# Low halves of 32 weight tiles written by ScalarE and an adding transfer instead of VectorE, and eight convolution slices per tile

## The chip, the core and the metric

The kernel runs on one core of a Trainium2 chip. The metric is the device time of one execution in microseconds (us). Engines are named as in the profile: PE (TensorE matrix multiplies), PEld (its weight loads), DVE (VectorE), ACT (ScalarE), POOL (GpSimd), SP (SyncE, which only issues transfers here).

## The reference, cut to what matters

One decoder layer over 1024 positions of width 1024, all in float32: a mixer (an input projection whose columns feed four heads of causal differential attention and a gated convolution of width 31), a cross-attention into 256 memory tokens, a gated feed-forward part and a final norm. The change touches only how the weights of the input projection and of the memory projection are prepared:

```
proj = jnp.einsum("bsd,dc->bsc", h, w_in)        # q, k, v and 2 x 512 convolution columns
c = u[..., :CV_WIDTH] * jax.nn.sigmoid(u[..., CV_WIDTH:])
c = causal_dwconv(c, cv_dw_w) + cv_dw_b          # width 31
...
kv = jnp.einsum("bmd,de->bme", m, w_ckv)         # 256 memory tokens, 2048 columns
```

## The kernel before, in words

Each float32 product is made of three passes on TensorE in the rounded format fp32r: a weight tile `raw` (128x1024, 512 KB) is split into `whi` (the value rounded to fp32r) and `wlo = raw - whi`, and `mm3` (L196 to L200) multiplies hi by lo, lo by hi and hi by hi. `split_w` (L174) makes the two halves: ACT copies raw into `whi` (L181), then DVE subtracts (L182). There are two buffers each of `whi` and `wlo` and three of `raw`, so the split of a tile can begin only when TensorE has finished the tile two places ahead of it, and it must be done when TensorE reaches the tile itself. `need(kind, m)` hands out a prepared tile and has the next one loaded (by SP, L171) and split.

The tiles come in the order of the list `seq`. The input projection has 16 ("in", order `in_order`; the first two are split in quarters by other code), then 4 for the values ("v", `vproj`), 16 for the memory ("kv", called kv0 to kv15 here, `mem_kv`, each 24 multiplies of 256 columns), and later "out", "cq", "co" and "dn".

The stages that matter:

- From about 60 to 232 us the projections run: one tile takes 48 multiplies of 512 columns. DVE meanwhile empties their results and runs the depthwise convolution `conv31`, cut into slices of one instruction of some 0.74 us (L371). `run_bg(NBG)` takes NBG slices after each tile, at a lower priority than the rest (17 such calls); `run_bg(1000)` takes what is left after `vproj`.
- From 232 to about 430 us the differential attention runs. TensorE's order is written out by hand: in each step scores (L695 to L698), transposes, weighted sums, and pieces of `mem_kv` as filler between them. DVE takes row maxima (L708), combines (L734 to L738) and empties the memory products (`mb`, L628; a single PSUM buffer, so the next pair of kv tiles waits for it). ACT takes exponentials (L714) and copies. POOL has small chains for norms (L779 to L783 and L814 to L816).

The order within ACT, DVE, POOL and SP is made by a scheduler ahead of time, from priorities and its own estimate of durations; on the chip each engine and each queue goes strictly in that order, and an instruction that waits holds up everything behind it.

Of the kernel before, what the change touches and what calls it, by code (L numbers as in the profile page):

```python
# [14 lines left out]
ALU = mybir.AluOpType  # L15
# [42 lines left out]
def hybrid_block_kernel(ctx: ExitStack, tc: tile.TileContext, xT, memT, pos, vecs, lams, ropec,  # L58
                        wi, wv, wo, wq, wkv, wc, wu, wd, gfin, outT, outB):
    nc = tc.nc  # L60
# [15 lines left out]
    def nm(s):  # L76
        cnt[0] += 1
        return f"{s}_{cnt[0]}"

    def R():  # L80
        return pt.tile([P, S], F32R, tag="t", name=nm("r"))
# [4 lines left out]
    def T(dt=F32):  # L86
        return pt.tile([P, S], dt, tag="t", name=nm("t"))
# [19 lines left out]
    def f(ap):  # L107
        return ap.bitcast(F32)
# [34 lines left out]
    in_order = [12, 8, 0, 1, 13, 9, 2, 3, 14, 10, 4, 5, 6, 7, 15, 11]  # L143
# [30 lines left out]
    def split_w():  # L174
        kind, m, mode, raw = loaded.pop(0)
        if mode == "rd":
            hi, lo = R(), R()
        else:
            hi = pw[0].tile([P, S], F32R, tag="whi", name=nm("whi"), bufs=2)
            lo = pw[0].tile([P, S], F32R, tag="wlo", name=nm("wlo"), bufs=2)  # L180
        nc.scalar.copy(out=hi, in_=raw)  # L181
        nc.vector.tensor_tensor(out=lo, in0=raw, in1=f(hi), op=ALU.subtract)  # L182
        prepped[(kind, m)] = (hi, lo)

    def need(kind, m, ahead=None):
# [5 lines left out]
    def load_to(i):  # L191
        while wpos[0] <= min(i, wend[0] - 1):
            load_w()
            split_w()
# [65 lines left out]
    for i in range(2):  # L260
        kind, m, src, _ = seq[wpos[0]]
        wpos[0] += 1
        raw = pw[0].tile([P, S], F32, tag="raw", name=nm("raw"), bufs=3)
# [67 lines left out]
    def run_bg(n):  # L331
        with tc.high_priority(offset=-500):
            while n > 0 and bg:
                g = bg.pop(0)
                if next(g, StopIteration) is not StopIteration:
                    bg.append(g)
                    n -= 1
# [117 lines left out]
    def rope(tiles):  # L455

        r = T()
        for h in range(NH):
            nc.scalar.dma_start(out=r[h * 32:(h + 1) * 32, :], in_=tiles[h][48:80, :])
        sw = T()  # L460
        nc.vector.stream_shuffle(out=sw, in_=r, mask=SWAP)
        nc.vector.tensor_tensor(out=r, in0=r, in1=cos_t, op=ALU.mult)
        nc.vector.tensor_tensor(out=sw, in0=sw, in1=sin_t, op=ALU.mult)
        nc.vector.tensor_tensor(out=r, in0=r, in1=sw, op=ALU.add)
        for h in range(NH):
            nc.scalar.dma_start(out=tiles[h][48:80, :], in_=r[h * 32:(h + 1) * 32, :])
# [38 lines left out]
                                           in1=rxb[:, sl], op0=ALU.mult, op1=ALU.mult)  # L505
        qk[m] = t

    NBG = 6

    with tc.manual_schedule(engines={mybir.EngineType.PE}):  # L510
        w, w2 = need("in", 12), need("in", 8, 0)
# [27 lines left out]
    for m in in_order[3:]:  # L539
# [6 lines left out]
        else:  # L546
            qk_out(m, [(slice(0, S), ps)])
            if m % 4 == 3:
                rope(qk[m - 3:m + 1])
        run_bg(NBG)  # L550
    vsb = [T() for _ in range(4)]

    def vproj():
# [3 lines left out]
        for i in range(4):  # L557
# [8 lines left out]
            if i < 3:  # L566
                run_bg(NBG)
        for tb in range(NB):
# [277 lines left out]
    next(prep)  # L846
    run_bg(NBG)

# [139 lines left out]
    for m in range(8):  # L988
# [8 lines left out]
        hi, lo = R(), R()  # L997
# [601 lines left out]
```

## Time and profile before

| | us |
|---|---|
| median of three runs | 1416.72 (1414.6 to 1417.54) |
| the profiled execution | 1418.36 |
| its span, first to last instruction | 1416.6 |
| busy: PE / DVE / ACT / POOL | 1378.1 / 1066.8 / 578.1 / 211.2 |

A busy time is the sum of an engine's instructions; matrix multiplies overlap one another, so a full PE stretch shows a busy time equal to its length. The granted clock of TensorE (PEclk) is 1.00 at 2.4 GHz and half of that at 1.2 GHz.

### The profile page before, as it was taken

Reading aid. Unit: us, or ns where it says so; the run is one execution under the profiler, and the core shown is the slowest. Engines: PE = TensorE matmul, PEld = TensorE weight load, DVE = VectorE, ACT = ScalarE, POOL = GpSimd, SP = SyncE. Lnnn points to the kernel's source line nnn. Section 1 sums busy time; section 2 is a strip of 40 time slices with the busy share of each in tenths; the row PEclk is TensorE's granted clock in tenths of the full one; section 3 lists DMA queues with packets and bytes.
Section 4 is the critical chain, followed back from the end, with each engine's and each line's share of the span. In section 5 each row is a group of like instructions: output and inputs, shape, how many; then the busy total and the mean of one; then the engine's idle time right before and its main releaser. Section 6 shows DMA issues by size and latency. Waiting matters only on the chain.

```text
span 1416.6 us, 17449 instructions
## 1 busy us (share of the span) xinstructions
PE 1378.1 (97%) x6709; PEld 1148.2 (81%) x6709; DVE 1066.8 (75%) x1385; ACT 578.1 (41%) x1023; POOL 211.2 (15%) x169
## 2 busy tenths in 40 slices
PE   8999999898899999999999999999999999999998
PEld 6888887887787888888878787887887877888886
DVE  7799999999955424454688888988888897666636
ACT  6211135688763223343464444444443451221213
POOL 0000000013210000000134333443334400000000
PEclk9999999999999999999999999999999999999999
DMA  6132123432205422202421222222222274313103
GB/s 220 42 98 73 56 90 98 141 118 77 74 31 200 149 90 74 75 31 75 155 80 70 76 80 83 89 75 79 85 75 89 89 299 176 119 61 118 45 1 119
DMA packets 50196, 137.36 MB, mean 97 GB/s; under 512 B 6336, under 2 KB 8640, under 8 KB 50112
## 3 DMA queue, kind: packets, MB, share of 16 engines
q1 hardware_dynamic: 43904, 119.98, 25.2%
q10 hardware_dynamic: 6208, 16.26, 3.6%
q8 instruction: 53, 0.87, 0.2%
q14 instruction: 31, 0.25, 0.1%
HBM read 101.51 MB, written 28.41 MB: 92 GB/s over the span
## 4 chain that ended last, share of the span: by engine, by line
PE 61%; DVE 18%; issue 8%; ACT 7%; POOL 6%; DMA 1%; SPq 0%; POOLq 0%; ACTq 0%; DVEq 0%
PE big L198 16%; PE big L200 16%; PE big L199 16%; POOL t L1171 5%; DVE q L1323 4%; ACT q L1321 3%; PE tb L765 2%; DVE r L221 2%; PE bk L198 1%; DVE wu L221 1%; PE bk L200 1%; PE bk L199 1%; PE mb L198 1%; DVE q L1346 1%; DVE q L1298 1%
## 5 line engine op out<-in xcount | busy, mean ns | idle before, releaser
L199 PE MATMUL big<-r,wlo 128*128 128x512 f32 x624 | 243.7, 390 | 0.6 <-DVE wlo L182 0.6
L200 PE MATMUL big<-r,whi 128*128 128x512 f32 x624 | 243.7, 391 | 0.0
L198 PE MATMUL big<-r,whi 128*128 128x512 f32 x560 | 219.7, 392 | 3.1 <-DVE r L304 2.1
L181 ACT CAST whi<-raw 128x1024 fp32r<-128x1024 f32 x58 | 61.4, 1058 | 204.1 <-PE big L200 171.2
L199 PEld LDWEIGHTS big<-r,wlo 128*128 128x128 f32 x624 | 117.6, 188 | 24.8 <-DVE wlo L182 0.9
L200 PEld LDWEIGHTS big<-r,whi 128*128 128x128 f32 x624 | 117.4, 188 | 24.6
L1431 DVE TENSOR_TENSOR t<-t,big 128x1024 f32<-128x1024 f32 x70 | 85.4, 1220 | 61.9 <-PE big L200 61.8
L1323 DVE SCALAR_TENSOR_TENSOR q<-q,vec,q 128x1023 f32<-128x1023 f32 x88 | 112.6, 1280 | 19.9 <-ACT q L1321 19.8
L198 PEld LDWEIGHTS big<-r,whi 128*128 128x128 f32 x560 | 105.6, 189 | 27.0 <-DVE r L304 3.4
L198 PE MATMUL big<-r,r 128*128 128x512 f32 x312 | 121.8, 391 | 1.8 <-DVE t L1431 1.6
L199 PE MATMUL big<-r,r 128*128 128x512 f32 x312 | 121.5, 389 | 0.0
L200 PE MATMUL big<-r,r 128*128 128x512 f32 x312 | 121.5, 389 | 0.0
L198 PE MATMUL ub<-r,wu 128*128 128x512 f32 x302 | 119.0, 394 | 1.7 <-ACT half L1278 1.7
L199 PE MATMUL ub<-r,wu 128*128 128x512 f32 x302 | 117.6, 389 | 0.0
L200 PE MATMUL ub<-r,wu 128*128 128x512 f32 x302 | 117.6, 389 | 0.0
L1171 POOL TENSOR_TENSOR t<-uraw 128x512 f32<-128x512 f32 x22 | 48.4, 2199 | 389.3 <-DMA uraw<-in_wu_dram 167.1
L198 PE MATMUL ub<-r,t 128*128 128x512 f32 x228 | 90.0, 395 | 4.2 <-ACT half L1278 2.8
L199 PE MATMUL ub<-r,t 128*128 128x512 f32 x228 | 88.8, 390 | 0.0
L200 PE MATMUL ub<-r,t 128*128 128x512 f32 x228 | 88.8, 389 | 0.0
L371 DVE SCALAR_TENSOR_TENSOR cv<-t,vec,cv 128x511 f32<-128x511 f32 (+14 forms) x120 | 84.2, 743 | 0.0
L181 ACT CAST r<-raw 128x1024 fp32r<-128x1024 f32 x22 | 22.9, 1051 | 134.8 <-PE big L198 134.5
L182 DVE TENSOR_TENSOR wlo<-raw,whi 128x1024 fp32r<-128x1024 f32 x58 | 70.9, 1223 | 6.8 <-ACT whi L181 6.6
(340 smaller groups left out, 3047.8 us busy)
## 6 DMA issues: line engine op xcount, KB each, us to landing
uraw<-in_wu_dram SPq DMA_DIRECT2D x88, 256.0 KB, 2.9
z_dr<-q SPq DMA_DIRECT2D x22, 512.0 KB, 2.6
raw<-in_wd_dram SPq DMA_DIRECT2D x22, 512.0 KB, 3.7
t<-z_dr SPq DMA_DIRECT2D x22, 512.0 KB, 4.8
raw<-in_wkv_dram SPq DMA_DIRECT2D x16, 512.0 KB, 3.7
raw<-in_wi_dram SPq DMA_DIRECT2D x14, 512.0 KB, 3.7
t<-h_dr SPq DMA_DIRECT2D x9, 512.0 KB, 10.0
kv_dr<-r SPq DMA_DIRECT2D x8, 512.0 KB, 3.5
```

What stands on the lines that cost most here:

```text
L181: nc.scalar.copy(out=hi, in_=raw)
L182: nc.vector.tensor_tensor(out=lo, in0=raw, in1=f(hi), op=ALU.subtract)
L198: nc.tensor.matmul(out, wh, xl, start=start, stop=False, **kw)
L199: nc.tensor.matmul(out, wl, xh, start=False, stop=False, **kw)
L200: nc.tensor.matmul(out, wh, xh, start=False, stop=stop, **kw)
L221: nc.vector.tensor_tensor(out=lo, in0=src, in1=f(hi), op=ALU.subtract)
L371: nc.vector.scalar_tensor_tensor(out=y[:, i:], in0=x[:, :n2 - i], scalar=t, in1=y[:, i:], op0=ALU.mult, op1=ALU.add)
L765: nc.tensor.matmul(av, u["at"][:, bs(j)], vsb[j // 2][:, (j % 2) * HALF + h * P:][:, :P], start=j == 0, stop=j == qb)
L1171: nc.gpsimd.tensor_tensor(out=out, in0=a, in1=b, op=ALU.add)
L1321: nc.scalar.mul(t, u, tp[2])
L1323: nc.vector.scalar_tensor_tensor(out=t[:, d:], in0=u[:, :S - d], scalar=tp[2 - d], in1=t[:, d:], op0=ALU.mult, op1=ALU.add)
L1431: nc.vector.tensor_tensor(out=h2[m], in0=h2[m], in1=ps, op=ALU.add)
```

## The change: what it does

For 32 tiles (the last 12 of "in", the 4 "v" and the 16 "kv") the subtraction on DVE is left out. ACT writes a second tile, `lo = -hi`, and a transfer issued from POOL's queue adds the raw tile to it on the way (`accum_op=ALU.add`), SBUF to SBUF, 512 KB. The sum is the same low half. POOL issued no transfer before. The other tiles keep the subtraction. NBG goes from 6 to 8.

```
         nc.scalar.copy(out=hi, in_=raw)
-        nc.vector.tensor_tensor(out=lo, in0=raw, in1=f(hi), op=ALU.subtract)
+        if kind in ("v", "kv") or kind == "in" and m not in in_order[:4]:
+
+            nc.scalar.mul(lo, f(hi), -1.0)
+            nc.gpsimd.dma_start(out=f(lo), in_=raw, accum_op=ALU.add)
+        else:
+            nc.vector.tensor_tensor(out=lo, in0=raw, in1=f(hi), op=ALU.subtract)
         prepped[(kind, m)] = (hi, lo)
...
-    NBG = 6
+    NBG = 8
```

## Rows read from the trace of the kernel before

**Rows 1.** Busy time by stage; columns: stretch, its length, busy (instructions), clock, DMA share, GB/s.
```profile
20.00:60.00 40.00, 40.00 (x194) 33.64 (x194) 30.15 (x59) 14.28 (x16) 1.67 (x1) 1.00 0.21 65
60.00:232.00 172.00, 172.00 (x766) 142.60 (x764) 164.17 (x243) 37.21 (x47) 0.00 (x0) 1.00 0.26 74
232.00:300.00 68.00, 60.74 (x453) 56.63 (x453) 64.24 (x98) 47.98 (x99) 3.32 (x3) 0.95 0.51 151
300.00:430.00 130.00, 119.18 (x841) 105.24 (x840) 104.31 (x206) 99.27 (x265) 32.90 (x62) 0.99 0.20 61
```

**Rows 2.** TensorE's waits, 232 to 300 us; total, times, longest.
```profile
PE mb L198 <- DVE half L628: 4.9, 3, 3.5
PE mb L198 <- DVE s L734: 2.3, 1, 2.3
```

**Rows 3.** TensorE's waits, 300 to 430 us: first and last of ten.
```profile
PE tb L822 <- ACT t L753: 2.8, 1, 2.8
...
PE tb L752 <- ACT junk L770: 0.2, 1, 0.2
```

**Rows 4.** Groups of instructions of the two halves; busy, mean ns, idle before.
```profile
L181 ACT CAST whi<-raw 128x1024 fp32r<-128x1024 f32 x58 | 61.4, 1058 | 204.1 <-PE big L200 171.2
...
L182 DVE TENSOR_TENSOR wlo<-raw,whi 128x1024 fp32r<-128x1024 f32 x58 | 70.9, 1223 | 6.8 <-ACT whi L181 6.6
```

**Rows 5.** Busy time by stage of the convolution's line L371 alone, DVE.
```profile
232.00:300.00 68.00, 11.07 (x15) 0.95 0.51 151
```

**Rows 6.** Timeline of ACT in the projections: start, length, instruction, idle before.
```profile
67.89 1.06 ACT L181 CAST whi<-raw 128x1024 fp32r<-128x1024 f32 x1 [9.78 <-PE big L200]
```

**Rows 7.** Timeline of ACT, the casts of kv1, kv2, kv4 and kv6.
```profile
231.83 1.04 ACT L181 CAST whi<-raw 128x1024 fp32r<-128x1024 f32 x1
...
236.12 1.06 ACT L181 CAST whi<-raw 128x1024 fp32r<-128x1024 f32 x1
...
249.41 1.05 ACT L181 CAST whi<-raw 128x1024 fp32r<-128x1024 f32 x1 [1.26 <-PE mb L200]
...
260.63 1.05 ACT L181 CAST whi<-raw 128x1024 fp32r<-128x1024 f32 x1 [4.99 <-PE mb L200]
```

**Rows 8.** Timeline of TensorE: kv1 starts, kv1 ends, kv2, kv2 ends, kv4, kv6.
```profile
236.21 0.36 PE L199 MATMUL mb<-r,wlo 128*128 128x256 f32 x1
...
238.93 0.28 PE L200 MATMUL mb<-r,whi 128*128 128x256 f32 x1
...
243.69 0.37 PE L198 MATMUL mb<-r,whi 128*128 128x256 f32 x1 [3.48 <-DVE half L628]
...
249.09 0.28 PE L200 MATMUL mb<-r,whi 128*128 128x256 f32 x1
...
255.13 0.55 PE L198 MATMUL mb<-r,whi 128*128 128x256 f32 x1 [2.32 <-DVE s L734]
...
266.65 0.39 PE L198 MATMUL mb<-r,whi 128*128 128x256 f32 x1 [0.67 <-DVE half L628]
```

**Rows 9.** Busy time in two stretches behind those stalls, all engines.
```profile
244.00:248.00 4.00, 4.00 (x21) 3.81 (x20) 3.94 (x5) 2.31 (x4) 0.00 (x0) 0.58 0.26 82
...
256.00:260.00 4.00, 4.00 (x24) 3.76 (x24) 4.00 (x11) 0.00 (x0) 0.00 (x0) 0.72 0.69 235
```

**Rows 10.** Timeline of DVE: a subtraction and the emptying of `mb` behind it.
```profile
252.18 1.22 DVE L182 TENSOR_TENSOR wlo<-raw,whi 128x1024 fp32r<-128x1024 f32 x1
...
254.30 0.69 DVE L628 TENSOR_TENSOR half<-mb,rmb 128x512 f32<-128x512 f32 x1
```

**Rows 11.** Transfers: SP's queue (packets, MB, share of 16 engines), then issues; KB, us to landing.
```profile
q1 hardware_dynamic: 43904, 119.98, 25.2%
...
z_dr<-q SPq DMA_DIRECT2D x22, 512.0 KB, 2.6
...
t<-h_dr SPq DMA_DIRECT2D x9, 512.0 KB, 10.0
```

**Rows 12.** Transfers, 228 to 300 us alone.
```profile
kv_dr<-r SPq DMA_DIRECT2D x4, 512.0 KB, 4.0
```

**Rows 13.** Timeline of POOL in the attention.
```profile
301.50 0.20 POOL L780 TENSOR_TENSOR s<-s,s 128x4 f32<-128x4 f32 x1 [10.06 <-ACT junk L770]
...
323.03 0.22 POOL L814 TENSOR_SCALAR s<-s 128x1 f32<-128x1 f32 x1 [11.31 <-DVE s L812]
...
326.01 1.25 POOL L814 TENSOR_SCALAR s<-s 128x1 f32<-128x1 f32 x1 [1.73 <-DVE s L812]
```

## The prediction, made before the change was run

> **What bounds the kernel now.** I read the busy times by stage first, because the 75% of DVE over the whole span is a mean over unlike stages. In the projections TensorE is full without a gap, 172.00 us of 172 at full clock, although DVE is also 95% busy (164.17) [rows 1]. So nothing that relieves DVE can shorten that stage: it can only be kept as it is. In the first part of the attention TensorE has 60.74 us of 68, with a clock of 0.95, and DVE 64.24: there DVE is the crowded engine. In the second part TensorE lacks 10.8 us of 130, DVE is at 80% and ACT at 76% [rows 1].
>
> The waits say what ends TensorE's gaps. Up to 300 us it is DVE alone: 4.9 + 2.3 = 7.2 us, always at a pair of kv tiles that waits for the emptying of `mb` [rows 2] (the row that names L734 is this too: the emptying at 254.30 had just ended, and it stood behind a subtraction at 252.18 [rows 8, 10]). After 300 us the ten entries sum to 10.5 us, 7.5 of them named for ACT and 3.0 for DVE [rows 3]. Behind the two longest stalls the granted clock was 0.58 and 0.72 for 4 us each, part of each stretch at 1.2 GHz instead of 2.4 [rows 9]: 4 x 0.42 + 4 x 0.28 = 2.8 us of work lost. So at most 7.2 + 2.8 = 10 us are to be had before 300 us, and a part of 10.5 after.
>
> **What leaves DVE.** 32 subtractions of 1.22 us [rows 4], 39 us. Seventeen (12 in, 4 v, kv0) lie before 232 us, 20.8 us, beside a full TensorE: worth nothing by themselves. The larger NBG brings 17 x 2 = 34 slices forward in the program, but only 15 slices, 11.07 us, still ran after 232 us [rows 5], so that is all that can leave the attention. The projections take them: 164.2 - 19.6 (the sixteen after 60 us) + 11.1 = 155.7 of 172 us. Slices have the lower priority, and a projection's results have a tile's time to be emptied in, so I cost the move at nothing; without the freed DVE it would be 11 us of DVE at the same place as now. In the attention DVE loses 15 subtractions (18.3 us) and these slices.
>
> **What ACT takes.** 32 second writes. The cast of the same size takes 1.06 us [rows 4], and I take that: 34 us. In the projections ACT has 37 us of 172 [rows 1], so they are hidden. From 232 to 430 us it is 15 x 1.06 = 16 us upon 147 of 198. The write stands right behind the cast, which already holds ACT for the same buffer (4.99 us at kv6 [rows 7]). What it delays are the exponentials and copies behind it. The 7.5 us of waits for ACT, grown in the share of 16 to 147, give +0.8; the ends are 0 and 15 x 1.06 = 16.
>
> **What the transfer costs.** This decides. Call X the time from the end of ACT's second write until TensorE may read `wlo`. The trace has neither an adding transfer nor one from POOL. The shortest 512 KB transfer lands in 2.6 us, the longest median is 10.0 [rows 11]; those are the ends. In this stage a 512 KB store takes 4.0 [rows 12]. An adding transfer must also read its target: SP's queue moved 119.98 MB in 25.2% of the span, 336 GB/s with all engines at work, so one more pass of 0.52 MB is 1.56 us. That gives 4.2 on an empty fabric and 5.6 on this stage's; I take 4.8, my estimate from these rows, with POOL's own time to issue it inside the spread.
>
> *In the projections* X is hidden: from the release of a buffer to its use lies one tile, 9.78 + 1.06 = 10.8 us [rows 6]; less two ACT instructions, 8.7 us are left. POOL's queue has nothing else there. SP frees a raw tile later by X, but with three of them that is a tile's time of slack.
>
> *In the attention* kv tiles follow one another faster than that. Now: release, cast 1.06, subtraction 1.22. Then: release, 2.12 on ACT, X. With X = 4.8:
> - kv1: cast at 231.83, so ready at 233.95 + 4.8 = 238.75; needed at 236.21 [rows 7, 8]. Late by 2.5. It ends 3.0 later (238.93 + 0.28 - 236.21), at 241.8, and 1.0 us of scores follow (to 243.69 - 3.48 now [rows 8]): 242.8.
> - kv2: the cast at 236.12 slips 1.06 behind kv1's write, so ready at 239.30 + 4.8 = 244.1, against 243.69 now. The stall of 3.48 has thus not gone; its cause has changed. Balance +0.4.
> - kv4: kv2 ends at 249.4 + 0.4; + 2.12 + 4.8 = 256.7, against 255.13 now: balance +1.6. The emptying itself would come about 2 us sooner without the subtraction ahead of it [rows 10], and that does not help.
> - kv6: kv4's end was the cast's start, 260.6, + 1.6 + 2.12 + 4.8 = 269.1, against 266.65: balance +2.4. From kv8 on the tiles are further apart.
>
> So the pairing of kv tiles costs +2.4 and takes back what DVE gives. By the same steps X = 3.5 gives -1.3, and with the slow stretches gone too, -4.1; X = 7 gives +9.
>
> The Trainium skill, "DMA: Bandwidth & Descriptors", section "Anatomy of one DMA — SWDGE (gpsimd) path", fits 2.0 us plus bytes over 436 GB/s for a transfer from POOL's queue, 3.2 us here as an estimate from that page, for a plain copy; with that as X the sum would turn to about -6. No row here shows such a transfer.
>
> **The rest of the attention.** After 267 us DVE has the eight subtractions of kv8 to kv15 (9.8 us) less. I credit 2.5 us, most of the 3.0 of waits named for DVE after 300 us [rows 3], and 0.5 for the third wait for `mb`; the ends are 0 and all 10.5.
>
> **The sum**: 2.4 - 2.5 - 0.5 + 0.8 = +0.2 us. Against the profiled execution, 1418.36 (span 1416.6 and 1.8 around it), that is 1418.6; it lay 1.6 above the median of the runs, so the median becomes 1416.9.
>
> **The rivals.**
> - *Short landing, faster.* X of 3.5 or less: the two stalls shrink, the slow stretches behind them vanish. -4.1 - 3.0 + 0.8 = -6.3: 1410.4. For it: the 2.6 us of the fastest row. Against it: the second read, and a busy fabric just there (0.51 [rows 1]).
> - *DVE was the queue of the whole attention, faster.* Then relief of 29 us of 169 shows also in waits named for ACT: the credit becomes 8 of the 10.5 instead of 2.5: 1416.9 - 5.5 = 1411.4. For it: DVE's 94% up to 300 us. Against: the names in [rows 3].
> - *Long landing, slower.* X of 7: +9 - 3.0 + 0.8 = +6.8: 1423.5; it decides from X of about 5.6, where the sum passes 0.2%. For it: 4.0 for a mere store in this stage [rows 12], and 10.0 elsewhere.
> - *POOL's queue blocks, slower.* POOL sits at L780 for 10.06 us and at L814 for 11.31 [rows 13]. A transfer put behind the first starts up to 10 us late; TensorE's use lies one tile behind the release, and at 301 us a kv tile with the attention's work around it takes some 5 to 7 us more than the 2.12 + X it needs, an estimate from 198 us of stage over 15 tiles: 3 to 5 are left, about 1421. For it: strict order. Against: from kv11 on there is time, and the order is made by expected readiness.
> - *POOL is starved by DVE, slower.* POOL's small instruction took 1.25 us instead of 0.22 beside a busy DVE [rows 13]. If issuing meets this again and again, X passes 8.7 even in the projections, and 16 tiles there lose each microsecond above it: X of 10 gives 16 x 1.3 + 20 = +41: about 1458. Against: one such delay is a microsecond, and there is one issue for a tile. I give it 0.04. The Trainium skill, "SBUF — State Buffer", section "SBUF: two separate sides", warns of this: while DVE runs an instruction in a mode with two ports, POOL cannot write a transfer's descriptors. No row here shows a transfer from POOL.
>
> **The numbers.** 0.2%, 2.8 us, is about what a measurement of this kernel can tell from no change. Within that: 0.30, X between 4.2 and 5.6, the likeliest case. Short landing 0.20 and DVE as the queue 0.16: faster 0.36. Long landing 0.22, POOL blocking 0.08, starved 0.04: slower 0.34. The range takes in the faster rivals with both together in part and the long landing up to X of about 8: 1406 to 1428, leaving out some 0.06 below and 0.12 above. The likeliest case's own range is 1414 to 1419.6.
>
> **What the profile after should show.** The projections full as before. No slice of L371 after about 235 us. kv1, kv2, kv4 and kv6 waiting for a transfer instead of DVE; the emptying of `mb` within a microsecond of its last multiply; X readable from the end of ACT's write to the first L199 of such a tile. Wrong would be: waits for `wlo` in the projections, POOL issuing for several microseconds, or kv tiles that never wait.

## The result, and the profile after

The changed kernel took 1439.3 us (median of 4 runs, 1438.39 to 1441.65) against 1416.45 for the kernel before on the same chip: a ratio of 1.0165, 95% interval 1.0148 to 1.0183, slower by 22.9 us. The forecast was 1416.9 with a range of 1406 to 1428. Line numbers behind L181 are larger by 5 from here on (`mm3` is L203 to L205, the emptying of `mb` L633, the convolution L376); L184 is ACT's second write, L185 the adding transfer, L187 the subtraction that is left.

The page of the changed kernel: busy times, the queue of POOL's transfers, and those transfers with the median time from issue to landing. Behind it, from the groups of instructions, the second write and the transfer's issue on POOL.

```profile
PE 1385.7 (96%) x6709; PEld 1154.8 (80%) x6709; DVE 1034.2 (72%) x1353; ACT 609.7 (42%) x1055; POOL 236.7 (16%) x201
...
q0 software_dynamic: 4608, 16.78, 6.1%
...
wlo<-raw POOLq DMA_DIRECT2D x32, 512.0 KB, 5.2
```

```profile
L184 ACT ACTIVATE wlo<-whi 128x1024 fp32r<-128x1024 f32 x32 | 34.1, 1064 | 0.6
...
L185 POOL DMA_DIRECT2D wlo<-raw x32 | 28.3, 884 | 234.7 <-ACT wlo L184 220.0 <-ACT t L758 14.3 <-ACT o L773 0.5
```

The work moved as the edit says. DVE's busy time fell by 32.6 us and ACT's grew by 31.6. A second write takes 1.06 us and one issue occupies POOL for 0.88 us.

Busy time by stage of the changed kernel, columns as in [rows 1]:

```profile
60.00:232.00 172.00, 168.03 (x735) 138.64 (x734) 155.79 (x236) 48.43 (x56) 12.89 (x15) 0.99 0.52 120
232.00:300.00 68.00, 51.38 (x327) 46.82 (x326) 29.68 (x49) 42.51 (x70) 7.64 (x9) 0.87 0.70 172
300.00:430.00 130.00, 117.02 (x883) 105.39 (x883) 105.05 (x215) 111.58 (x292) 35.15 (x63) 0.99 0.42 109
```

The middle row is the case in one line. From 232 to 300 us DVE went from 64.24 us to 29.68, and TensorE, which the relief was to feed, from 60.74 to 51.38. The DMA share rose from 0.51 to 0.70 and the granted clock fell from 0.95 to 0.87. One row up TensorE, full before, lacks 4.0 us.

TensorE's waits in the changed kernel name the transfer first. From 60 to 232 us, then from 232 to 300 us, as [rows 2], then the first line from 300 to 430 us:

```profile
PE bk L203 <- DMA wlo<-raw: 4.0, 1, 4.0
```

```profile
PE mb L204 <- DMA wlo<-raw: 14.3, 7, 4.6
PE mb L203 <- DVE half L633: 2.3, 3, 0.9
```

```profile
PE mb L204 <- DMA wlo<-raw: 3.8, 2, 2.3
```

The waits for DVE up to 300 us fell from 7.2 us to 2.3, and 14.3 us of waits for the transfer stand in their place. TensorE's timeline shows where: v0, then the first multiply with `wlo` of kv1, kv2, kv3, kv4, kv5 and kv7 (kv6 waits 0.15 us).

```profile
190.98 0.50 PE L203 MATMUL bk<-wlo,r 128*128 128x512 f32 x1 [3.97 <-DMA wlo<-raw]
...
246.24 0.58 PE L204 MATMUL mb<-r,wlo 128*128 128x256 f32 x1 [4.59 <-DMA wlo<-raw]
...
252.50 0.39 PE L204 MATMUL mb<-r,wlo 128*128 128x256 f32 x1 [0.20 <-DMA wlo<-raw]
...
260.22 0.38 PE L204 MATMUL mb<-r,wlo 128*128 128x256 f32 x1 [3.53 <-DMA wlo<-raw]
...
267.57 0.58 PE L204 MATMUL mb<-r,wlo 128*128 128x256 f32 x1 [1.00 <-DMA wlo<-raw]
...
275.82 0.38 PE L204 MATMUL mb<-r,wlo 128*128 128x256 f32 x1 [2.30 <-DMA wlo<-raw]
...
290.42 0.39 PE L204 MATMUL mb<-r,wlo 128*128 128x256 f32 x1 [2.51 <-DMA wlo<-raw]
```

The wait is not at the tile's first multiply, which needs `whi`, but at L204, its first multiply with `wlo`: ACT's cast was done (at kv1 at 238.24, when the wait began at 241.65). Each wait delays the release of a buffer, so the next tile's cast starts later too, and the waits add up. Against the kernel before, TensorE starts kv0 5.4 us later, kv2 8.3, kv4 11.1, kv6 15.0, kv8 19.7, kv10 22.2 and kv15 22.7. The 5.4 us at kv0 contain v0's wait of 3.97.

How kv1 was prepared, in ACT's timeline, then POOL's, then that one transfer (median of one):

```profile
237.20 1.04 ACT L181 CAST whi<-raw 128x1024 fp32r<-128x1024 f32 x1
238.26 1.04 ACT L225 CAST r<-q 64x1024 fp32r<-64x1024 f32 x1
239.33 1.06 ACT L184 ACTIVATE wlo<-whi 128x1024 fp32r<-128x1024 f32 x1
```

```profile
240.68 0.89 POOL L185 DMA_DIRECT2D wlo<-raw  x1 [1.57 <-ACT wlo L184]
```

```profile
wlo<-raw POOLq DMA_DIRECT2D x1, 512.0 KB, 5.5
```

From the cast's start to TensorE's read it is 246.24 - 237.20 = 9.0 us: cast 1.04, another piece of ACT's work in between 1.09, the write 1.06, the way to POOL 0.29, the transfer 5.5. The forecast had 2.12 + 4.8 = 6.9. For kv3 the same stretch is 9.1 us (251.11 to 260.22), for kv4 11.0 (256.61 to 267.57).

The clock behind the new waits, in two stretches:

```profile
186.00:196.00 10.00, 6.03 (x20) 4.50 (x19) 6.19 (x10) 7.07 (x11) 0.07 (x1) 0.83 0.59 154
...
244.00:252.00 8.00, 5.76 (x29) 5.42 (x29) 4.21 (x4) 4.72 (x6) 0.86 (x1) 0.60 0.72 172
```

In the 8 us that take in the last 2.2 us of kv1's wait of 4.59 and the work behind it, the granted clock was 0.60, most of it at 1.2 GHz; in [rows 9] it was 0.58 for 4 us. The clock is a part of the loss in its own right. From 232 to 300 us TensorE is busy 9.4 us less than before (51.38 against 60.74), and a clock of 0.87 instead of 0.95 over 68 us costs up to 5.4 us more; kv8 starts 14.4 us later, counted from kv0. Over whole executions the mean granted clock was 0.988 to 0.993 in the changed kernel and 0.993 to 0.998 in the one before.

### The profile page after: what moved, and what is told of

It reads as the page before. It is cut to its first block, busy times and chain, and to the rows that moved or that the text cites. A ratio compares the mean times of both kernels' runs of the same rounds, so it can differ in the third digit from the quotient of the medians.

```text
span 1439.5 us, 17558 instructions
## 1 busy us (share of the span) xinstructions
PE 1385.7 (96%) x6709; PEld 1154.8 (80%) x6709; DVE 1034.2 (72%) x1353; ACT 609.7 (42%) x1055; POOL 236.7 (16%) x201
## 4 chain that ended last, share of the span: by engine, by line
PE 60%; DVE 14%; issue 9%; ACT 8%; POOL 5%; DMA 4%; SPq 0%; POOLq 0%; ACTq 0%; DVEq 0%
PE big L203 15%; PE big L204 15%; PE big L205 15%; POOL t L1176 5%; DVE q L1328 4%; ACT q L1326 3%; DMA wlo<-raw 3%; PE tb L770 1%; PE bk L203 1%; PE bk L205 1%; PE bk L204 1%; DVE r L226 1%; DVE t L226 1%; PE ub L203 1%; PE ub L204 1%
## 5 line engine op out<-in xcount | busy, mean ns | idle before, releaser
L204 PE MATMUL big<-r,wlo 128*128 128x512 f32 x624 | 243.8, 391 | 0.6 <-DVE wlo L187 0.6
L205 PE MATMUL big<-r,whi 128*128 128x512 f32 x624 | 243.5, 390 | 0.0
L203 PE MATMUL big<-r,whi 128*128 128x512 f32 x560 | 219.9, 393 | 3.0 <-DVE r L309 1.9
L181 ACT CAST whi<-raw 128x1024 fp32r<-128x1024 f32 x58 | 61.2, 1054 | 193.3 <-PE big L205 159.7
L204 PEld LDWEIGHTS big<-r,wlo 128*128 128x128 f32 x624 | 117.6, 189 | 24.8 <-DVE wlo L187 0.9
L205 PEld LDWEIGHTS big<-r,whi 128*128 128x128 f32 x624 | 117.6, 188 | 24.6
L203 PEld LDWEIGHTS big<-r,whi 128*128 128x128 f32 x560 | 105.5, 188 | 26.6 <-DVE r L309 2.9
L1328 DVE SCALAR_TENSOR_TENSOR q<-q,vec,q 128x1023 f32<-128x1023 f32 x88 | 112.5, 1279 | 19.8 <-ACT q L1326 19.7
L203 PE MATMUL big<-r,r 128*128 128x512 f32 x312 | 121.9, 391 | 1.8 <-DVE t L1436 1.6
L204 PE MATMUL big<-r,r 128*128 128x512 f32 x312 | 121.6, 390 | 0.0
L205 PE MATMUL big<-r,r 128*128 128x512 f32 x312 | 121.5, 389 | 0.0
L203 PE MATMUL ub<-r,wu 128*128 128x512 f32 x302 | 119.3, 395 | 1.7 <-ACT half L1283 1.7
L205 PE MATMUL ub<-r,wu 128*128 128x512 f32 x302 | 118.3, 392 | 0.0
L204 PE MATMUL ub<-r,wu 128*128 128x512 f32 x302 | 118.2, 391 | 0.0
L203 PE MATMUL ub<-r,t 128*128 128x512 f32 x228 | 89.9, 394 | 3.8 <-ACT half L1283 2.2
L205 PE MATMUL ub<-r,t 128*128 128x512 f32 x228 | 88.8, 389 | 0.0
L204 PE MATMUL ub<-r,t 128*128 128x512 f32 x228 | 88.8, 389 | 0.0
L376 DVE SCALAR_TENSOR_TENSOR cv<-t,vec,cv 128x511 f32<-128x511 f32 (+14 forms) x120 | 83.1, 734 | 0.1
L181 ACT CAST r<-raw 128x1024 fp32r<-128x1024 f32 x22 | 22.9, 1051 | 134.9 <-PE big L203 134.6
L713 DVE TENSOR_REDUCE s<-big 128x1 f32<-128x1024 f32 (+7 forms) x48 | 45.6, 953 | 38.5 <-PE big L703 38.3
```

Source lines behind the costliest of these rows:

```text
L203: nc.tensor.matmul(out, wh, xl, start=start, stop=False, **kw)
L204: nc.tensor.matmul(out, wl, xh, start=False, stop=False, **kw)
L205: nc.tensor.matmul(out, wh, xh, start=False, stop=stop, **kw)
L376: nc.vector.scalar_tensor_tensor(out=y[:, i:], in0=x[:, :n2 - i], scalar=t, in1=y[:, i:], op0=ALU.mult, op1=ALU.add)
L713: nc.vector.tensor_reduce(out=out, in_=src, axis=AX.X, op=ALU.max, negate=True)
L1328: nc.vector.scalar_tensor_tensor(out=t[:, d:], in0=u[:, :S - d], scalar=tp[2 - d], in1=t[:, d:], op0=ALU.mult, op1=ALU.add)
```

## The experiments

Each diff is against the changed kernel.

### Which tiles cost it: four parts alone

**In and v tiles with the transfer, kv tiles back on DVE (e1):**

```
-        if kind in ("v", "kv") or kind == "in" and m not in in_order[:4]:
+        if kind == "v" or kind == "in" and m not in in_order[:4]:
```

> The twelve in tiles and the four v tiles keep the adding transfer and NBG = 8; the kv tiles go back to DVE. If the loss is the landing of kv tiles (17 us of it) and one late first v tile (4.0 us of waiting and a slow clock behind it), this is about 1418 to 1422, with the 4 us wait of the first v tile still there. If the loss came from ACT's load or the slices of the convolution in the projections, it stays above 1430.

Measured: 1415.99 us, before 1416.51, ratio 0.9993 (0.9983 to 1.0003). The kv tiles are thus worth 1439.3 - 1416.0 = 23.3 us of the change. That is 2 us below what was expected, with the wait at v0 still there. TensorE's longest waits from 140 to 300 us:

```profile
PE bk L203 <- DMA wlo<-raw: 4.2, 1, 4.2
PE mb L203 <- DVE half L633: 2.6, 3, 1.2
```

**kv tiles alone, NBG 6 (e2):**

```
-        if kind in ("v", "kv") or kind == "in" and m not in in_order[:4]:
+        if kind == "kv":
...
-    NBG = 8
+    NBG = 6
```

> Only the sixteen kv tiles take the adding transfer, NBG = 6. Landing of kv tiles: about 1434, with some 18 us of waits of TensorE for kv transfers. If the in and v tiles or NBG were the cause: 1425 or less.

Measured: 1432.97 us, ratio 1.0109 (1.0094 to 1.0124): 16.5 us slower than before. Its waits from 232 to 300 us are those of the whole change:

```profile
PE mb L204 <- DMA wlo<-raw: 14.2, 7, 4.6
PE mb L203 <- DVE half L633: 2.3, 3, 0.9
```

**NBG 8 alone (e3):** all tiles subtract on DVE, `NBG = 8`.

> The kernel before with NBG = 8 alone. By either theory of the transfers: within 2 us of 1416.5. If the order that NBG makes were the cause: well above 1420.

Measured: 1416.49 us against 1416.51, ratio 1.0002 (0.9992 to 1.0011). The convolution's last slice ran at 267.0 us: without the freed DVE the slices are handed out earlier and run no earlier.

**The 12 in tiles alone, NBG 8 (e4):**

```
-        if kind in ("v", "kv") or kind == "in" and m not in in_order[:4]:
+        if kind == "in" and m not in in_order[:4]:
```

> Only the twelve in tiles take the adding transfer, NBG = 8. Landing theory: no wait for a transfer in the projections, since a tile's time of 10.8 us covers two ACT instructions and 6 to 7 us; the first v tile, on DVE again, is ready in time; and the attention finds less convolution left: 1411 to 1417. If the transfers themselves disturb (raw tiles freed late, fabric shared): above 1419.

Measured: **1409.14 us** (1407.92 to 1411.69), ratio 0.9945 (0.993 to 0.996): faster than both kernels, by 7.4 us than the one before, and below the 1411 to 1417 expected. Its busy times by stage and its waits from 232 to 300 us:

```profile
60.00:232.00 172.00, 172.00 (x774) 142.92 (x773) 161.50 (x241) 49.15 (x58) 8.88 (x11) 1.00 0.43 108
232.00:300.00 68.00, 63.58 (x501) 59.15 (x500) 61.34 (x98) 52.15 (x117) 5.79 (x11) 1.00 0.51 156
```

```profile
PE mb L203 <- DVE half L633: 3.1, 3, 1.7
PE mb L203 <- ACT whi L181: 1.3, 1, 1.3
```

The projections are full, no slice runs after 232 us, the longest stall went from 3.5 us to 1.7, and the clock is 1.00 throughout. So the transfers of the in tiles are hidden (they land in 4.5 us here, and no multiply waits for one), and the 11 us of convolution, all that leaves DVE in the attention here, do pay there: TensorE is busy 2.8 us longer from 232 to 300 us (63.58 against 60.74), and the clock of 1.00 instead of 0.95 gives back up to 3.4 us of these 68.

The four runs do not simply add. The in tiles gain 7.4 us; the v tiles cost 1415.99 - 1409.14 = 6.9; the kv tiles cost 16.5. With the gain that makes 16.0, against 22.9 measured for the whole; without it, 6.9 + 16.5 = 23.4. This fits a gain that is lost where the kv tiles wait for transfers instead of DVE. That it is lost entirely is read out of this sum, not measured by itself.

### What a kv tile's cost is made of

**ACT's second write, and DVE's addition in place of the transfer, for the kv tiles (e9);** the in tiles as in e4, v on DVE:

```
-            nc.gpsimd.dma_start(out=f(lo), in_=raw, accum_op=ALU.add)
+            if kind == "kv":
+                nc.vector.tensor_tensor(out=lo, in0=raw, in1=f(lo), op=ALU.add)
+            else:
+                nc.gpsimd.dma_start(out=f(lo), in_=raw, accum_op=ALU.add)
```

> The in tiles take the adding transfer; the kv tiles have ACT write the negative half too, but DVE adds raw to it: ACT's load of the change without the transfer's landing; v tiles on DVE as before. Landing theory: near the kernel with the in tiles alone (1409), plus 1 to 4 for sixteen more ACT instructions. If ACT's load is what hurts the attention: 1420 or more.

Measured: 1416.94 us, ratio 1.0009 (0.9998 to 1.0019), 7.8 us over e4, where 1 to 4 were expected. No kv tile uses a transfer here and DVE has as much to do as in e4, so this is the price of the longer chain without a landing: a second write on ACT, with whatever ACT does between the two, and DVE's addition behind it in DVE's own order (at kv2 it begins at 243.17, 1.9 us after the write ended). Of the 23.3 us that the kv tiles cost, about 15 are then left for the landing in place of a 1.22 us instruction, if the two prices add. TensorE's waits of e9 from 232 to 300 us (its `mm3` is at L206 to L208):

```profile
PE mb L207 <- DVE wlo L186: 3.5, 2, 3.3
PE mb L206 <- ACT wlo L184: 2.5, 1, 2.5
```

**The second write without its wait for the cast (e5):** ACT writes -raw, rounded, in place of -hi; the rest as in the change.

```
-            nc.scalar.mul(lo, f(hi), -1.0)
+            nc.scalar.mul(lo, raw, -1.0)
```

> All 32 tiles as in the change, but ACT writes the negative half from raw and not from the cast's result, so that it need not wait for the cast and other work of ACT need not come between them (1.0 to 1.4 us did, at kv1 to kv4). Landing theory, with every microsecond of the chain counting at the nine kv tiles that wait: 8 to 12 us less than the change, about 1428 to 1431. If only the landing itself or contention counts: no change, 1439.

Measured: 1432.69 us, ratio 1.012 (1.0096 to 1.0143), 6.6 us less than the change, just short of what was expected. (At kv3 only 0.4 us of other work stood between cast and write, not 1.0.) ACT's order changes with it, so this is no clean price of one wait. From 140 to 300 us the kv tiles wait 5.8 us for transfers instead of 14.3, and a v tile still waits:

```profile
PE mb L204 <- DMA wlo<-raw: 5.8, 3, 2.5
PE big L203 <- DMA wlo<-raw: 4.8, 1, 4.8
PE mb L203 <- DVE half L633: 4.3, 4, 2.0
```

**A transfer that copies and doesn't add (e7):** `accum_op=ALU.add` left out.

> The transfer from POOL's queue copies raw without adding (the low halves are then wrong by the high ones). If the addition's second read is what makes the landing long, it falls from 5.2 us by about 1.5, and the nine waits by about 13 us: 1425 to 1428. If the way through POOL is the price: landing stays near 5, and the time near 1439.

Measured: 1429.3 us, ratio 1.009 (1.0073 to 1.0107), 10 us less than the change and just above the 1425 to 1428 expected; the waits of the kv tiles fell from 18.0 us to 11.4, not by 13. The landings of e7, from 60 to 170 us and then from 232 to 300 us:

```profile
wlo<-raw POOLq DMA_DIRECT2D x11, 512.0 KB, 2.9
```

```profile
wlo<-raw POOLq DMA_DIRECT2D x9, 512.0 KB, 4.5
```

In the change they are 4.6 and 5.9 us in the same stretches. The addition costs 1.7 us of landing in the projections and 1.4 in the attention; the forecast's estimate for a second read was 1.56. A landing is counted from the start of the issue, and the issue takes 0.86 us for the adding transfer and 0.53 for the plain one, so up to 0.3 of it may be the issue and not the read.

**The same plain copy from SP's queue (e8):** `nc.sync.dma_start(out=f(lo), in_=raw)`.

> As the run that copies the raw tile without adding it, on all tiles of the change, but from SP's queue in place of POOL's (the low parts are then wrong: the addition is left out). Theory 'what costs is the time that the bytes need to land, whoever issues': the landing stays near 3.4 us and the time near 1429.3. Rival 'issuing from POOL (0.86 us an issue, and the way from ACT to it) is a good part of the stall': about 1 us less for each of nine stalls, 1420 to 1423. Second rival, SP's queue is in order and its next loads stand behind the wait for ACT: loads come late, over 1435.

Measured: 1418.89 us, ratio 1.0023 (1.0013 to 1.0032), 10.4 us less than the same copy from POOL. No theory has it whole. The time is nearest to the rival that blames the way through POOL, and below its range. But the landing did stay, as the first theory said: the median of e8's copies, from 60 to 170 us and then from 232 to 300 us (the trace has the landing of 23 of the 32), is near that of e7's, 2.9 and 4.5:

```profile
wlo<-raw SPq DMA_DIRECT2D x10, 512.0 KB, 3.2
```

```profile
wlo<-raw SPq DMA_DIRECT2D x11, 512.0 KB, 4.6
```

Nor did nine stalls shrink by 1 us each: seven kv tiles wait 11.4 us in e7, and seven wait 9.8 in e8. (No multiply waited for a load of SP's, against the second rival.) What e8 saves besides is that no v tile waits, where in e7 v0 and v1 wait 3.4 us, and the clock. The same stretch in e7, then in e8:

```profile
232.00:300.00 68.00, 55.68 (x392) 50.81 (x391) 37.24 (x59) 51.41 (x88) 5.94 (x11) 0.95 0.65 202
```

```profile
232.00:300.00 68.00, 55.67 (x425) 50.74 (x424) 40.13 (x64) 54.34 (x99) 2.24 (x3) 1.00 0.72 226
```

TensorE is busy equally long, at 1.00 instead of 0.95, up to 3.4 us of work. The three come to at most 8.4 of the 10.4 us.

Single tiles differ more. kv1's transfer in e8, then in e7:

```profile
wlo<-raw SPq DMA_DIRECT2D x1, 512.0 KB, 3.2
```

```profile
wlo<-raw POOLq DMA_DIRECT2D x1, 512.0 KB, 4.8
```

From the end of ACT's write to the read it is 3.26 us (234.01 to 237.27) against 5.12 (240.17 to 245.29). Of the 1.9 us between them 0.27 is the way to the issuing engine (0.02 us to SP, 0.29 to POOL) and the rest the landing. This is the widest pair: at kv5 the two are 5.44 and 6.39, at kv10 6.15 and 5.99. Both copies of kv1 meet 256 KB transfers `r<-r` from SP's queue. One of them is issued behind the copy in e8 (234.56, the copy at 234.03), while in e7 the copy, from another queue, has two of them just ahead and alongside (239.11 and 240.41, the copy at 240.46). v0 is alike: in e7 its copy is issued at 184.07, beside a load from SP at 184.11, and lands in 5.8 us; in e8 the load is issued 0.57 us behind the copy, in the same queue, and the copy lands in 3.2. That SP's one queue puts the copy ahead of later traffic, while POOL's shares the engines with it, fits this, and no run tests it by itself; a start that is later with every transfer of POOL's does not fit the medians. The waits of e8 show that a plain copy from SP's queue doesn't hide either.

The Trainium skill, "DMA: Bandwidth & Descriptors", section "Anatomy of one DMA — SWDGE (gpsimd) path", has a fit that makes 3.2 us of a plain transfer of this size, an estimate from that page. e7 agrees in the projections (2.9), and not in the attention (4.5).

### The v tile, and the last kv tiles

**v0 back on DVE, v1 to v3 with the transfer, kv on DVE (e10):**

```
+        if kind == "v" and m > 0 or kind == "in" and m not in in_order[:4]:
```

> In tiles and the last three v tiles take the adding transfer; the first v tile and the kv tiles go through DVE. If the 6.9 us between the runs with and without the v tiles is the first of them alone, which is late because ACT stands waiting for the memory's transfer: near 1409. If the v tiles as such are too close for the landing: near 1416.

Measured: 1416.96 us, ratio 1.0008 (0.9998 to 1.0017). That is the time of the second theory, but v2 and v3 do not wait. The stall was not taken away, it moved to v1:

```profile
200.88 0.50 PE L203 MATMUL big<-wlo,r 128*128 128x512 f32 x1 [4.13 <-DMA wlo<-raw]
```

What stands ahead of a v tile's write is the load of the memory, which takes raw buffers as well. ACT's timeline of the changed kernel, SP's wait for that load from 140 to 260 us before and after the change, and v0's transfer:

```profile
176.21 1.06 ACT L591 ACTIVATE acc<-memr 128x1024 f32<-128x1024 f32 x1 [8.78 <-DMA memr<-in_memT_dram]
...
180.83 1.04 ACT L181 CAST whi<-raw 128x1024 fp32r<-128x1024 f32 x1
...
182.72 1.06 ACT L184 ACTIVATE wlo<-whi 128x1024 fp32r<-128x1024 f32 x1
...
188.54 1.15 ACT L594 ACTIVATE half<-memr 128x512 f32<-128x512 f32 x2 [4.76 <-DMA memr<-in_memT_dram]
```

```profile
SPq L582 <- DVE wlo L182: 20.3, 2, 10.5
```

```profile
SPq L587 <- DMA wlo<-raw: 10.5, 1, 10.5
```

```profile
wlo<-raw POOLq DMA_DIRECT2D x1, 512.0 KB, 6.9
```

SP stood 10.5 us at this load before the change too, until DVE's subtraction had read the raw tile. Now an adding transfer must have read it, and the load is issued at 172.30 instead of 169.50. ACT, in its order, stands 8.78 us at the first use of the load (L591; 6.62 before) with v0's cast behind it: the cast starts at 180.83, where before it started at 176.69. A cast for the memory (L225) comes between v0's cast and its second write, which ends at 183.78. The transfer lands 6.9 us after its issue, against 4.6 for the in tiles, and v0, needed at 187.0, is read at 190.98. In e8 the same transfer lands in 3.2 us and v0 doesn't wait. With v0 on DVE v1 stands in the same place: its cast, behind the second load (L594), starts at 190.85, where before it started at 187.57, and its transfer lands in 6.8 us. So it takes a v tile with a transfer behind a delayed load, and the cure that was run is e4's: no v tile with a transfer. There the load is late too, issued at 170.92, and v0 has only a subtraction behind its cast.

**The last five kv tiles with the transfer as well (e11);** in tiles as in e4:

```
+        if kind == "kv" and m > 10 or kind == "in" and m not in in_order[:4]:
```

> The in tiles take the adding transfer, and so do kv11 to kv15; kv0 to kv10 and v keep the subtraction; slices 8 a tile. Theory 'the landing costs where kv tiles follow one another closely': the whole change ran 22.2 us later than before at kv10 and 22.7 at kv15, so the last five transfers cost about 0.5 and give DVE 5 x 1.22 us: 1407 to 1411, against 1409.1 with the in tiles alone. Rival 'every kv transfer costs its share of the 23.3 us': 5 of 15 tiles, about 7.8 us, 1417.

Measured: 1408.54 us (1408.17 to 1410.95), ratio 0.9955 (0.9942 to 0.9969), not to be told from e4. No multiply waits for a transfer. Where kv tiles lie far apart the transfer costs nothing that these runs can tell, and what it takes from DVE there gains nothing that they can tell either. e4, with less in it, is the version to keep.

## Why the prediction was wrong

**The mechanism was among the rivals; its size was not.** The rival "long landing" came true in kind: kv tiles wait for the transfer in place of DVE. It had a chance of 0.22 and a price of 1423.5, 16 us short.

**The step that failed first: "What the transfer costs", X = 4.8.** At the nine kv tiles that waited X was 5.7 to 7.9 us: 5.85 for kv1, 5.7 for kv2, 6.6 for kv3 and 7.9 for kv5. Its parts: the second read was estimated well (1.56, measured 1.4 to 1.7). The plain landing was not: I took 2.6 to 4.0 us from rows of SP's queue, and in the attention e7's copies took 4.5. That they come from POOL's queue is not the reason, since e8's copies from SP's took 4.6 there. I also took the DMA engines as in this stage before, at a share of 0.51 [rows 1]; with the new transfers it is 0.70, and no run shows how much of X that makes. X alone is not the whole miss: with X = 7 the prediction's own steps gave +6.8 us, and 22.9 were measured.

**The second: "The write stands right behind the cast."** It does so for the in tiles. In the attention, but for kv8, 0.4 to 2.2 us of ACT's other work stands between them, 1.09 at kv1. From the cast's start to the use kv1 to kv5 and kv7 take 9.0 to 11.0 us, not 6.9. The term for ACT, +0.8, counted what its 16 us delay behind them; the write's place in the chain of a kv tile is where it cost, 7.8 us in e9 with DVE's addition behind it.

**The third: only kv2, kv4 and kv6 were counted, and no slow clock behind the new waits.** I took the stall of kv1 as one that ends in the gap before kv2, and let the tiles from kv8 on be far enough apart. All of kv1 to kv7 waited, and kv9 and kv10 again (2.33 and 1.42 us): each late tile makes the next release later, and the chain has no slack to give it back. The +9 worked out for X = 7 was thus too small as well: the start of kv8 is 19.7 us late, 14.4 of them since kv0. Slow stretches entered the working only as something to be saved; the clock went from 0.95 to 0.87 over 68 us, up to 5.4 us.

**The fourth: "SP frees a raw tile later by X, but with three of them that is a tile's time of slack."** No weight load made TensorE wait. But SP had no slack at the memory's load, which takes a raw buffer from the same three and where it stood waiting before the change too; that load came 2.8 us later, with ACT's v tile standing behind it. The v tiles cost 6.9 us, the slow clock behind the wait among it (0.83 over the 10 us from 186 to 196), and neither the sum nor a rival had it.

**The credits, 2.5 + 0.5, and what they hang on.** After 300 us the waits named for DVE, 3.0 us, are gone in the changed kernel, while those named for ACT went from 7.5 to 8.9. The third wait for `mb` is as long as before (0.67 us at kv6), so the 0.5 was not there. What DVE's relief can be worth shows in e4: 7.4 us, near the time of the rival that put "DVE was the queue of the whole attention" (1411.4), but not by its road: in e4 the waits after 300 us sum to 10.6 us, as before (10.5). NBG 8 without the relief brings none of it, and the relief with NBG 6 was not run. The subtractions of the last five kv tiles bring nothing that e11 can tell, and where TensorE waits for `wlo`, a DVE with 29.68 us of work in 68 helps nobody.

**What was right.** The in tiles' transfers are hidden behind a tile's time of 10.8 us: they land in 4.6 (median; one in 7.05). NBG alone is nothing. No slice ran after 232 us. POOL's queue did not block: but for one of 0.49 us, every issue from 183 to 318 us began 0.3 us after ACT's write. Nor was POOL starved: an issue took 0.86 to 0.95 us in the attention and 0.85 to 0.86 in the projections after 60 us, beside a DVE that was busy 91% of that stage; here the trace shows nothing of the warning on descriptors in the Trainium skill, "SBUF — State Buffer", section "SBUF: two separate sides". Whether any DVE instruction here runs in the mode that it speaks of, no row shows. Waits for the emptying of `mb` fell to 0.9 us at most.

**What stays open.** Why the same plain copy lands in 2.8 to 2.9 us at one tile of the attention and in 6.1 at another, with either queue; other traffic on the DMA engines at that moment fits the pairs that were looked at. Why the clock fell further behind these waits than behind those of before, and not at all in e8. And whether an adding transfer with a third pair of `whi` and `wlo` would hide in the attention, which wasn't run.

## What to carry to other kernels

Taking work off a busy engine helps only if what replaces it is ready as early: where a tile has 10.8 us from release to use, a 5 us transfer for a 1.2 us instruction is free, and where the tiles follow one another in 3 to 8 us it is a wait at each of them, and each wait delays the next. Split such a change by stage before judging it: here the same edit was worth -7.4 us on the tiles of one stage and +16.5 on those of another. And count every user of the source buffer, which a transfer holds until it lands: here a load of something else came 2.8 us later, and the preparation of a v tile stood behind that load on ACT.

## What the runs showed of the hardware that was not expected

- A 512 KB copy from SBUF to SBUF issued by POOL landed in 2.9 us in the projections and 4.5 in the attention (e7, medians); the adding one in 4.6 and 5.9, up to 7.6. POOL is busy 0.53 us for the issue of the plain one and 0.86 for the adding one (0.95 at most in the attention); SP's issue took 0.47.
- The same copy from SP's queue landed in 3.2 and 4.6 us (e8, medians). At kv1 it reached TensorE 1.9 us earlier than from POOL's, at kv10 0.2 us later.
- A wait of 4.59 us at kv1 was followed by work at 1.2 GHz (a mean of 0.60 from 244 to 252 us), and one of 3.97 us at v0 by a mean of 0.83 from 186 to 196 us. With waits of 1.7 us at most (e4) the clock stayed at 1.00 through both stages, and in e8, with waits of up to 2.36 us, it did so too; in the kernel before a wait of 2.32 us was followed by 0.72 for 4 us [rows 9].
